# Conditioning summed along rows of output channels, with its products placed behind the weight tiles' low halves

## The chip, the cores and the metric

The kernel runs on one core of one Trainium2 chip. The metric is the device time of one execution in microseconds (us); lower is better. Inputs and output are float32 in the chip's main memory.

## The reference, cut to what matters

One decoder layer on 256 tokens of 2048 channels. A vector `c` (one per sequence) conditions it through a 2048 x 12288 matrix `w_ada`: six rows of 2048 values, which are a shift, a scale and a gate for each of the two sub-layers.

```python
mod = silu(c) @ w_ada + b_ada            # 6 x 2048: shift, scale, gate, shift, scale, gate
h = layer_norm(x) * (1 + mod[1]) + mod[0]
proj = h @ w_in                          # 2048 -> 9760 columns, in one product
...                                      # sparse attention and matrix memory on parts of proj
x = layer_norm(ALPHA * x + mod[2] * (merged @ w_o))
h = layer_norm(x) * (1 + mod[4]) + mod[3]
a, g = split(h @ w_up)
x = layer_norm(ALPHA * x + mod[5] * ((silu(dwconv(a)) * g) @ w_down))
```

The first norm inside each sub-layer has no gain and bias; the one after the residual has them.

## The kernel before, in words

Every weight tile is 128 partitions x 1024 float32 (512 KB; 392 KB for the `w_in_a` tiles of 784 columns). `load` issues it on SP's queue into one of the buffers of tile `w`; `load_split` then makes two halves of it for TensorE's reduced float32: ScalarE casts the high half (`wh`, line 96), VectorE subtracts to get the low half (`wl`, line 97). Each product is three matmuls: high by high, high by low, low by high. There are 4 buffers each of `wh` and `wl` and, before the change, 6 of `w` (`WB`).

**Conditioning.** `w_ada` is 192 such tiles, 32 for each of the six rows. A tile of `w_ada` holds 128 *input* channels on its partitions and 1024 outputs in its columns. VectorE multiplies each tile by one value per partition and adds it to an accumulator `acc` (line 157, one dependent chain of 16 tiles), after which TensorE sums over the partitions: for shifts and scales by matmuls against ones into `ps_ada`, for gates into `ps_adar`. The first 512 channels' shift and scale go straight from `ps_ada` into `modc` (one value per partition and chunk); later ones are copied to a row by ScalarE and moved onto the partitions by two small DMAs (`raw<-row`). So that a chunk is ready in this layout, channels are taken in a turned order: chunk 4 q + i, partition p is channel 512 q + 4 p + i. The transposes of the normalised input (`turn`) and the second norm's output `n2` therefore read or write with a stride of four elements.

**Input projection.** The 16 chunks of 128 input channels are taken in four groups of four. In each group the kernel runs over all columns of `w_in`: 24 blocks of 128 columns by `mm_b` (bank `ps_b`), then six ranges of 392 or 512 columns by `mm_a` (`ps_a`). A group has 24 weight tiles, 6 for each chunk. Its results are copied out by ScalarE in group 0 and added to the earlier ones by VectorE in the later groups. A group can begin only when shift and scale of its chunks are known and `hm` (ScalarE, line 299), the high cast of `hT` (ScalarE, 301) and its low half (VectorE, 302) are made.

**Ticker.** All other conditioning is spread over the weight tiles: after each weight tile `tk.tick(rate)` runs that many steps of a queue of generators; a step loads one `w_ada` tile and adds it to `acc` at once. During group g the ticker prepares group g + 1, one tile after each of the first weight tiles. The second sub-layer's shift and scale (64 tiles) start in group 3, the gates (32 tiles each) in the branch projections and in the channel mixer.

What is written here fixes the work and its data flow; a scheduler then sets the order in which the instructions stand in each engine's queue. Each engine takes its queue in order. `manual_schedule` around the norm between the sub-layers keeps VectorE's and ScalarE's written order there.

After the input projection come the merge gates' products, which fill the time between the steps of attention and matrix memory, the branch projections, the output projection, two norms, and the channel mixer in two halves (`ps_up`, `ps_d`).

Of the kernel before, what the change touches and what calls it, by code (L numbers as in the profile page):

```python
# [14 lines left out]
P = 128  # L15
S = 256
# [16 lines left out]
GR = (1.0, 1.0)  # L33
# [3 lines left out]
WB = (6, 4, 4)  # L37
NG0 = 8
FIRST = 14
F0 = 1  # L40
PTV = 2
YA, YB = 1, 2
# [9 lines left out]
def build(ctx: ExitStack, tc: tile.TileContext, d, out, dbg=None):  # L52
# [15 lines left out]
    nc.sync.dma_start(cst, d["cst"])  # L68
    ident = cst[:, C_ID:C_ID + P]
# [20 lines left out]

    def load_split(src):
# [5 lines left out]
        nc.vector.tensor_sub(wl[:, :n], t[:, :n], wh[:, :n])  # L97
        return wh, wl
# [24 lines left out]
    def rstd_steps(var, out_ap, n, nm):  # L123
        """1/sqrt(var + EPS), with a Newton step after the table's square root."""
# [20 lines left out]
    # ---------------------------------------------------------------- conditioning  # L145
# [4 lines left out]
    def ada_partial(u):  # L150
        acc = p0.tile([P, 1024], F32, name="acc", tag="acc")
        for k in range(KD):
            t = load(d["w_ada"][u * KD + k])
            if k == 0:
                nc.vector.tensor_scalar(acc, t, cs[:, 0:1], None, op0=ALU.mult)
            else:
                nc.vector.scalar_tensor_tensor(acc, t, cs[:, k:k + 1], acc, op0=ALU.mult, op1=ALU.add)  # L157
            if k < KD - 1:
                yield
        yield acc  # L160

    def ada_cols(u, m_sh, m_sc, q):
        """Shift and 1 + scale of the channels 512 q + 4 p + i, on partition p, in column 4 q + i."""
        for acc in ada_partial(u):
            if acc is None:
                yield
        for _ in range(YA):
            yield
        ps = bank(psa, "ps_ada")
        if q == 0 and m_sh == 0:  # L170
            src = [ps[:, 4 * i:4 * i + 4] for i in range(2)]
            for i in range(2):
                v = acc[:, i * 512:(i + 1) * 512].rearrange("k (c b) -> k b c", b=4)
                for b in range(4):
                    mm(src[i][:, b:b + 1], v[:, b, :], ones[:, 0:1], True, True)
        else:
            raw = p0.tile([P, 2, 4], F32, name="raw", tag="raw", bufs=2)
            for i in range(2):
                mm(ps[32 * i:32 * i + 32, :], ones[:, 0:32], acc[:, i * 512:(i + 1) * 512], True, True)
            row = t2([64, 512], "row")  # L180
            nc.scalar.copy(row, ps[0:64, :])
            for i in range(2):
                nc.scalar.dma_start(raw[:, i, :], row[32 * i:32 * i + 1, :])
            src = [raw[:, i, :] for i in range(2)]
            for _ in range(YB):
                yield
        for i, m in ((0, m_sh), (1, m_sc)):
            c0 = m * KD + 4 * q
            nc.vector.tensor_add(modc[:, m, 4 * q:4 * q + 4], src[i],
                                 prm[:, R_BADA + c0:R_BADA + c0 + 4])  # L190
        nc.vector.tensor_scalar(modc[:, m_sc, 4 * q:4 * q + 4], modc[:, m_sc, 4 * q:4 * q + 4],
                                1.0, None, op0=ALU.add)
        yield

    def ada_rows(u, dst, col, c):
        """1024 gate values on every partition."""
        for acc in ada_partial(u):
            if acc is None:
                yield
        for i in range(2):  # L200
            c0 = c * 1024 + i * 512
            bt = t2([P, 512], "badar")
            nc.sync.dma_start(bt, d["b_ada"][0:1, col + c0:col + c0 + 512].to_broadcast([P, 512]))
            ps = bank(psa, "ps_adar")
            mm(ps, ones, acc[:, i * 512:(i + 1) * 512], True, True)
            nc.vector.tensor_add(dst[:, c0:c0 + 512], ps, bt)
        yield

    def run_all(g):
        for _ in g:  # L210
            pass

    class Ticker:
        def __init__(self):
            self.q, self.credit = [], 0.0
# [3 lines left out]

        def tick(self, n):  # L220
# [9 lines left out]
        def drain(self):  # L230
            while self.q:
# [5 lines left out]
    # ---------------------------------------------------------------- input norm  # L237
# [4 lines left out]
    xt = p0.tile([P, 2, D], F32, name="xt", tag="t16")  # L242
    for t in range(2):
        for c in (0, 1024):
            nc.sync.dma_start(xt[:, t, c:c + 1024], d["x"][t * P:(t + 1) * P, c:c + 1024])
# [22 lines left out]
    first = ada_cols(0, 0, 1, 0)  # L268
    for _ in range(FIRST):
        next(first)  # L270
# [10 lines left out]
    def turn(p):  # L281
        ps = bank(psa, "ps_nT")
        for i in range(2):
            for t in range(2):
                q, b = divmod(2 * p + i, 4)
                v = xt[:, t, q * 512:(q + 1) * 512].rearrange("s (c b) -> s b c", b=4)
# [919 lines left out]
```

## Time and profile before

| | us |
|---|---|
| median of 3 runs | 1524.73 |
| lowest, highest run | 1518.71, 1528.0 |
| span of the profiled execution | 1516.5 |
| TensorE busy in it | 1457.4 |
| VectorE busy | 1112.6 |
| ScalarE busy | 727.0 |

For the profiled execution the page gives its span, from the first to the last instruction, and no time of its own beside it; the median of the runs is 8.2 us above that span, the lowest run 2.2 us.

The page's first part gives each engine's busy time, the second the span in 40 slices, the fourth the chain of work that ended last, followed back from the end. A share of busy time is an average over stages with different limits, so the questions that matter are which engine runs without a break in a given stretch and what ends its breaks; a matmul's end is modelled, so that counts of matmuls over a stretch say more than TensorE's busy share.

### The profile page before, as it was taken

To read this page: it belongs to the slowest core of one execution; us is meant where nothing else is said; L and a number is where in the kernel's file an instruction comes from. 1 tells how busy PE (TensorE), PEld (TensorE's weight loads), DVE (VectorE), ACT (ScalarE), POOL (GpSimd) and SP (SyncE) were. 2 spreads that over 40 slices of the span, in tenths; PEclk is the share of its full clock that TensorE was granted. 3 is DMA by queue.
4 is the path that set the end of the run, shared out by engine and by line. 5 is a ranking of instruction groups with operands and counts; after the bars stand their busy time and mean duration, and the time that the engine had idled before them with its cause. 6 is when DMAs were issued, how large, how long until landed. Compare 5 with 4: busy or idle time off the path is not lost.

```text
span 1516.5 us, 23668 instructions
## 1 busy us (share of the span) xinstructions
PE 1457.4 (96%) x9174; PEld 1299.5 (86%) x9174; DVE 1112.6 (73%) x1478; ACT 727.0 (48%) x1031; POOL 2.1 (0%) x6
## 2 busy tenths in 40 slices
PE   1999999999999999999699999999999999999997
PEld 1999898888889999988688888888898888888887
DVE  7869896897868778868877888865556666665557
ACT  3663443556565443434465455553335555554341
POOL 0000000000000000000000000000000000000000
PEclk9999999999999999999899999999999999999999
DMA  9989888894858899998358888866666666666662
GB/s 365 324 284 333 290 316 274 304 339 134 313 160 309 284 324 330 330 355 298 138 184 279 281 287 275 275 186 192 195 192 195 187 188 185 188 184 191 192 196 87
DMA packets 106961, 376.98 MB, mean 249 GB/s; under 512 B 13792, under 2 KB 13920, under 8 KB 106080
## 3 DMA queue, kind: packets, MB, share of 16 engines
q1 hardware_dynamic: 104832, 375.43, 73.9%
q8 instruction: 72, 1.18, 0.3%
q10 hardware_dynamic: 2016, 0.03, 0.1%
q14 instruction: 41, 0.34, 0.1%
HBM read 373.29 MB, written 2.10 MB: 248 GB/s over the span
## 4 chain that ended last, share of the span: by engine, by line
PE 89%; DVE 6%; DMA 2%; issue 1%; ACT 1%; DVEq 0%; SPq 0%; ACTq 0%
PE ps_up L77 33%; PE ps_d L77 16%; PE ps_mg L77 12%; PE ps_b L77 7%; PE ps_br L77 6%; PE ps_o L77 5%; PE ps_a L77 5%; DMA w<-in_w_ada_dram 2%; DVE acc L157 2%; DVE wl L97 1%; PE ps_y L77 1%; PE ps_s L77 1%; PE ps_ada L77 1%; PE ps_hid L77 1%; DVE xz L890 1%
## 5 line engine op out<-in xcount | busy, mean ns | idle before, releaser
L96 ACT CAST wh<-w 128x1024 fp32r<-128x1024 f32 (+1 forms) x478 | 495.9, 1038 | 571.4 <-PE ps_d L77 124.0
L97 DVE TENSOR_TENSOR wl<-w,wh 128x1024 fp32r<-128x1024 f32 (+1 forms) x478 | 575.4, 1205 | 255.1 <-ACT wh L96 254.7
L77 PE MATMUL ps_up<-h2T,wh 128*128 128x512 f32 x1408 | 496.5, 398 | 0.0
L77 PE MATMUL ps_up<-h2T,wl 128*128 128x256 f32 x1408 | 393.7, 280 | 0.0
L77 PEld LDWEIGHTS ps_up<-h2T,wh 128*128 128x128 f32 x1408 | 265.1, 188 | 64.3 <-ACT wh L96 0.5
L157 DVE SCALAR_TENSOR_TENSOR acc<-w,cs,acc 128x1024 f32<-128x1024 f32 x180 | 230.7, 1282 | 56.5 <-DMA w<-in_w_ada_dram 55.0
L77 PEld LDWEIGHTS ps_up<-h2T,wl 128*128 128x128 f32 x1408 | 266.0, 189 | 0.6 <-issue 0.5
L77 PE MATMUL ps_d<-wh,uTt 128*128 128x512 f32 (+1 forms) x792 | 210.4, 354 | 0.0
L77 PE MATMUL ps_mg<-hT,wh 128*128 128x256 f32 x1024 | 192.4, 287 | 0.0
L77 PEld LDWEIGHTS ps_mg<-hT,wh 128*128 128x128 f32 x1024 | 161.8, 193 | 5.7 <-issue 4.9
L77 PEld LDWEIGHTS ps_d<-wh,uTt 128*128 128x128 f32 x792 | 140.4, 189 | 20.8
L77 PE MATMUL ps_mg<-hT,wl 128*128 128x256 f32 x512 | 146.1, 285 | 0.0
L77 PE MATMUL ps_b<-hT,wh 128*128 128x256 f32 x768 | 140.4, 284 | 1.4 <-ACT hT L301 0.7
L77 PE MATMUL ps_d<-wl,uTt 128*128 128x512 f32 (+1 forms) x396 | 140.0, 354 | 0.0
L77 PEld LDWEIGHTS ps_b<-hT,wh 128*128 128x128 f32 x768 | 119.9, 192 | 5.9 <-issue 3.9
L77 PE MATMUL ps_b<-hT,wl 128*128 128x256 f32 x384 | 108.6, 283 | 0.6 <-DVE wl L97 0.6
L77 PE MATMUL ps_a<-wh,hT 128*128 128x392 f32 (+1 forms) x384 | 109.1, 359 | 0.0
L77 PEld LDWEIGHTS ps_mg<-hT,wl 128*128 128x128 f32 x512 | 98.6, 193 | 0.8 <-issue 0.7
L77 PEld LDWEIGHTS ps_d<-wl,uTt 128*128 128x128 f32 x396 | 74.9, 189 | 10.3
L77 PEld LDWEIGHTS ps_a<-wh,hT 128*128 128x128 f32 x384 | 71.0, 188 | 10.0 <-issue 2.7
L77 PEld LDWEIGHTS ps_b<-hT,wl 128*128 128x128 f32 x384 | 73.6, 192 | 1.2 <-DVE wl L97 0.8
L77 PE MATMUL ps_a<-wl,hT 128*128 128x392 f32 (+1 forms) x192 | 68.6, 358 | 0.0
(248 smaller groups left out, 1400.6 us busy)
## 6 DMA issues: line engine op xcount, KB each, us to landing
w<-in_w_ada_dram SPq DMA_DIRECT2D x192, 512.0 KB, 4.9
w<-in_w_up_dram SPq DMA_DIRECT2D x176, 512.0 KB, 4.2
w<-in_w_down_dram SPq DMA_DIRECT2D x90, 512.0 KB, 3.9
w<-in_w_mg_dram SPq DMA_DIRECT2D x64, 512.0 KB, 5.0
w<-in_w_in_b_dram SPq DMA_DIRECT2D x48, 512.0 KB, 5.0
w<-in_w_br_dram SPq DMA_DIRECT2D x32, 512.0 KB, 5.4
w<-in_w_o_dram SPq DMA_DIRECT2D x32, 512.0 KB, 5.5
w<-in_w_in_a_dram SPq DMA_DIRECT2D x32, 392.0 KB, 4.3
```

The source lines that it names most:

```text
L77: nc.tensor.matmul(o, lhsT, rhs, start=start, stop=stop)
L96: nc.scalar.copy(wh[:, :n], t[:, :n])
L97: nc.vector.tensor_sub(wl[:, :n], t[:, :n], wh[:, :n])
L157: nc.vector.scalar_tensor_tensor(acc, t, cs[:, k:k + 1], acc, op0=ALU.mult, op1=ALU.add)
L890: nc.vector.scalar_tensor_tensor(z, z, mv[:, 0:1], lg[:, c * 512:(c + 1) * 512], op0=ALU.subtract, op1=ALU.mult)
```

## The change: layout and sum, groups, placing, buffers

1. `w_ada` is stored transposed: a tile now holds 128 *output* channels on its partitions and half of the 2048 input channels in its columns. `crow` holds silu(c) along the free axis, the same on every partition; 16 transposes and 4 ScalarE copies make it at the start. One VectorE instruction multiplies a tile by half of `crow` and sums along the columns (`accum_out`) into `parts`. Two halves and the bias are added, and `modc` is there: no `acc` chain, no `ps_ada`, no small DMAs. A chunk of 128 channels is ready after 4 tiles (shift and scale, two halves each).
2. Channels are taken in plain order: the strides of four in `turn` and `second_norm` go.
3. The gates come out per partition too. After two more ticks (`YA`) they are spread by 8 transposes of 128 columns and 2 ScalarE copies per 1024 gates; before it was two ones matmuls of 512 columns in two passes each, a bias load and two VectorE additions.
4. The groups of the projection are 3, 4, 5 and 4 chunks. The rate of the ticker in a group is set so that the `w_ada` tiles of the next group are spread evenly over all its weight tiles (16 over 18, 20 over 24, 16 over 30).
5. A tick now loads the tile; the product is written at the next tick, after that weight tile's low half, and `behind` forbids the scheduler to move it in front of that.
6. `w` has 8 buffers. The input `x` is loaded ahead of everything but the constants, as it already was in the queue.

```diff
+GROUPS = (3, 4, 5, 4)
-WB = (6, 4, 4)
+WB = (8, 4, 4)
...
+        lows.append(nc.vector.tensor_sub(wl[:, :n], t[:, :n], wh[:, :n]))
...
+        nc.tensor.transpose(ps[:, j * P:(j + 1) * P], cs[:, 4 * i + j:4 * i + j + 1].to_broadcast([P, P]),
+                            ident)
+    nc.scalar.copy(crow[:, i * 512:(i + 1) * 512], ps)
...
+    def ada_chunk(m, k):
+        for i in range(2):
+            t = load(d["w_ada"][(m * KD + k) * 2 + i])
+            def products(t=t, i=i):
+                ins = nc.vector.scalar_tensor_tensor(
+                    t, t, 1.0, crow[:, i * 1024:(i + 1) * 1024], op0=ALU.mult, op1=ALU.mult,
+                    accum_out=parts[:, m, k, i:i + 1])
+                if lows:
+                    behind(ins, lows[-1])
+            yield products
...
+        def last():
+            products()
+            o, v = modc[:, m:m + n, k0:k1], parts[:, m:m + n, k0:k1, :]
+            nc.vector.tensor_add(o, v[:, :, :, 0], v[:, :, :, 1])
+            nc.vector.tensor_add(o, o, bada[:, m:m + n, k0:k1])
+            if then:
+                then()
...
+    def ada_mod(k0, k1):
+        while k0 < k1:
+            k = min(k0 + 2, k1)
+            yield from ada_cols(0, 2, k0, k, lambda k0=k0, k=k: modulate_in(k0, k))
+            k0 = k
+    run_all(ada_mod(0, GROUPS[0]))
...
         def tick(self, n):
+            self.flush()
             self.credit = self.credit + n if self.q else 0.0
             while self.credit >= 1 and self.q:
                 self.credit -= 1
                 try:
-                    next(self.q[0])
+                    f = next(self.q[0])
+                    if f:
+                        self.late.append(f)
...
+    for gi, kn in enumerate(GROUPS):
+        nxt = gi < len(GROUPS) - 1
+        if nxt:
+            tk.add(ada_mod(k0 + kn, k0 + kn + GROUPS[gi + 1]))
+            rate = 4 * GROUPS[gi + 1] / (6 * kn)
...
     def second_norm(t, c):
-        z = xz[:, t, c * 512:(c + 1) * 512].rearrange("s (c b) -> s c b", b=4)
-        o = n2[:, t, c * 512:(c + 1) * 512].rearrange("s (b c) -> s c b", b=4)
+        z, o = xz[:, t, c * 512:(c + 1) * 512], n2[:, t, c * 512:(c + 1) * 512]
```

How the instructions move, at three places.

SP's queue at the start, before:

```order
L245 DMA xt<-in_x_dram 128x1024 x4
L88 DMA w<-in_w_ada_dram 128x1024 x6
L407 DMA gb<-in_ml_gate_b_dram 128x8
L88 DMA w<-in_w_ada_dram 128x1024 x10
L88 DMA w<-in_w_in_b_dram 128x1024
L88 DMA w<-in_w_ada_dram 128x1024
L88 DMA w<-in_w_in_b_dram 128x1024
```

The same place with the change:

```order
L72 DMA xt<-in_x_dram 128x1024 x4
L92 DMA w<-in_w_ada_dram 128x1024 x8
L415 DMA gb<-in_ml_gate_b_dram 128x8
L92 DMA w<-in_w_ada_dram 128x1024 x4
L92 DMA w<-in_w_in_b_dram 128x1024 x2
L92 DMA w<-in_w_ada_dram 128x1024
L92 DMA w<-in_w_in_b_dram 128x1024
```

The first weight tile moves from the 17th to the 13th place among the large tiles.

ScalarE's queue where group 0 ends and group 1 begins, before (the numbers at `ps_a` are banks; the last range of group 0 is 917 and 918):

```order
L96 CAST wh<-w 128x1024
L299 ACTIVATE hm<-nT,modc 128x256 x4
L301 CAST hT<-hm 128x2x256
L96 CAST wh<-w 128x1024
L301 CAST hT<-hm 128x2x256
L530 COPY projA<-ps_a_872 128x2x256
L530 COPY projA<-ps_a_873 128x2x256
L96 CAST wh<-w 128x1024 x2
L530 COPY projA<-ps_a_917 128x2x256
L530 COPY projA<-ps_a_918 128x2x256
```

With the change (the last range of group 0 is 772 and 773):

```order
L537 COPY projA<-ps_a_732 128x2x256
L537 COPY projA<-ps_a_733 128x2x256
L107 CAST wh<-w 128x1024
L537 COPY projA<-ps_a_772 128x2x256
L107 CAST wh<-w 128x1024
L537 COPY projA<-ps_a_773 128x2x256
L310 ACTIVATE hm<-nT,modc 128x256 x2
L107 CAST wh<-w 128x1024
L312 CAST hT<-hm 128x2x256
```

All four chunks of group 1 were modulated ahead of group 0's last copies; now its last two chunks are modulated behind the copy of group 0's last bank.

VectorE's queue at the same place with the change:

```order
L108 TENSOR_TENSOR wl<-w,wh 128x1024
L180 SCALAR_TENSOR_TENSOR w,parts<-w,crow 128x1024 x2
L108 TENSOR_TENSOR wl<-w,wh 128x1024
L198 TENSOR_TENSOR modc<-parts 128x2x2
L108 TENSOR_TENSOR wl<-w,wh 128x1024
L199 TENSOR_TENSOR modc<-modc,prm 128x2x2
L108 TENSOR_TENSOR wl<-w,wh 128x1024
L180 SCALAR_TENSOR_TENSOR w,parts<-w,crow 128x1024
L313 TENSOR_TENSOR hT<-hm,hT 128x2x256
```

The last two products of group 1's conditioning stand behind group 0's last low half (the first row), and the low half of `hT` behind three low halves of group 1.

## Rows read from the trace of the kernel before

**Rows 1.** Windows: stretch, its us, busy us (instructions) by engine, PEclk, DMA share, GB/s.

```profile
0.00:45.70 45.70, 11.39 (x52) 10.02 (x52) 34.23 (x51) 18.08 (x29) 1.16 (x5) 1.00 0.95 355
45.70:80.00 34.30, 34.30 (x286) 34.30 (x287) 27.82 (x25) 18.26 (x26) 0.00 (x0) 1.00 0.94 334
327.00:465.90 138.90, 138.77 (x931) 117.74 (x931) 105.99 (x177) 81.48 (x178) 0.00 (x0) 0.98 0.66 232
```

**Rows 2.** The chain that ended last, in order: start us, us, what.

```profile
33.57 1.30 DVE acc L157
34.91 3.90 PE ps_ada L77 x16
...
40.27 2.08 ACT hm L299 x4
...
88.70 0.98 PE ps_ada L77 x4
...
173.91 34.57 PE ps_b L77 x286
208.48 14.10 PE ps_a L77 x79
...
237.70 7.67 PE ps_b L77 x64
...
406.55 0.87 PE ps_pT L684 x8
...
567.89 1.72 PE ps_adar L77 x4
```

**Rows 3.** Timeline, start and joint of groups 0 and 1: start us, us, engine, line.

```profile
17.73 17.13 DVE L157 SCALAR_TENSOR_TENSOR acc<-w,cs,acc 128x1024 f32<-128x1024 f32 x13
...
33.78 1.05 ACT L96 CAST wh<-w 128x1024 fp32r<-128x1024 f32 x1 [12.05 <-DMA w<-in_w_in_b_dram]
...
109.16 0.40 PE L77 MATMUL ps_b<-hT,wh 128*128 128x256 f32 x2
```

**Rows 4.** VectorE from 109 to 174 us, by shape: busy us, mean ns, idle before.

```profile
L97 DVE TENSOR_TENSOR wl<-w,wh 128x1024 fp32r<-128x1024 f32 x16 | 19.4, 1219 | 0.0
L157 DVE SCALAR_TENSOR_TENSOR acc<-w,cs,acc 128x1024 f32<-128x1024 f32 x15 | 19.2, 1283 | 5.1 <-DMA w<-in_w_ada_dram 5.0
L97 DVE TENSOR_TENSOR wl<-w,wh 128x784 fp32r<-128x784 f32 x8 | 7.7, 975 | 0.0
...
L501 DVE TENSOR_TENSOR accM<-ps_b,accM 128x512 f32<-128x512 f32 x4 | 2.8, 691 | 0.0
...
L302 DVE TENSOR_TENSOR hT<-hm,hT 128x512 fp32r<-128x512 f32 x2 | 1.3, 684 | 0.0
...
L189 DVE TENSOR_TENSOR modc<-raw,prm 128x4 f32<-128x4 f32 x2 | 0.3, 158 | 4.5 <-DMA raw<-row 4.5
```

**Rows 5.** The norm between the sub-layers, 738 to 774 us, by shape.

```profile
L890 DVE SCALAR_TENSOR_TENSOR xz<-xz,mv_z,lnr 128x512 f32<-128x512 f32 x8 | 5.9, 741 | 0.0
L922 ACT ACTIVATE sqj<-xz,sq 128x512 f32<-128x512 f32 x8 | 5.6, 707 | 6.2 <-DVE sq L920 6.2
L895 DVE SCALAR_TENSOR_TENSOR xz<-xz,mv_z,lnr 128x512 f32<-128x512 f32 x8 | 5.6, 742 | 0.0
...
L947 ACT ACTIVATE n<-xz,mv_n 128x512 f32<-128x512 f32 x4 | 5.1, 1272 | 0.0
...
L895 DVE DVE_READ_ACCUMULATOR xz<-xz,mv_z,lnr 128x1 f32 x8 | 0.7, 82 | 0.0
```

**Rows 6.** ScalarE over the whole program, by shape.

```profile
L299 ACT ACTIVATE hm<-nT,modc 128x256 f32<-128x256 f32 x16 | 8.3, 593 | 4.3 <-DVE modc L191 4.3
...
L301 ACT CAST hT<-hm 128x512 fp32r<-128x512 f32 x8 | 4.8, 618 | 0.0
...
L530 ACT COPY projA<-ps_a 128x512 f32<-128x512 f32 x4 | 2.2, 588 | 1.1 <-PE ps_a L77 1.0
```

**Rows 7.** DMA from 16 to 34 us: packets, MB, mean rate.

```profile
DMA packets 2153, 7.32 MB, mean 407 GB/s; under 512 B 367, under 2 KB 367, under 8 KB 2153
```

More of the change, by code (lines that the diff above doesn't have):

```diff
@@ L68, in build @@
     nc.sync.dma_start(cst, d["cst"])
+    xt = p0.tile([P, 2, D], F32, name="xt", tag="t16")
+    for t in range(2):
+        for c in (0, 1024):
+            nc.sync.dma_start(xt[:, t, c:c + 1024], d["x"][t * P:(t + 1) * P, c:c + 1024])
     ident = cst[:, C_ID:C_ID + P]
@@ L89, in load, with behind @@
         return t
+    lows = []
+    def behind(ins, other):
+        tc.add_manual_dep(ins.ins, other.ins.name, mybir.DependencyInfo(
+            mybir.DependencyClass.NoSync, mybir.DependencyReason.DATA), reason="order")
     def load_split(src):
@@ L148, in build @@
     modc = p0.tile([P, 6, KD], F32, name="modc")
[L150 to L166, printed above, removed]
+    parts = p0.tile([P, 6, KD, 2], F32, name="parts")
+    bada = prm[:, R_BADA:R_BADA + 6 * KD].rearrange("p (m k) -> p m k", m=6)
+    for m in (1, 4):
+        nc.vector.tensor_scalar(bada[:, m, :], bada[:, m, :], 1.0, None, op0=ALU.add)
+    crow = p0.tile([P, D], F32, name="crow")
+    for i in range(4):
+        ps = bank(psm, "ps_c")
+        for j in range(4):
+            nc.tensor.transpose(ps[:, j * P:(j + 1) * P], cs[:, 4 * i + j:4 * i + j + 1].to_broadcast([P, P]),
+                                ident)
+        nc.scalar.copy(crow[:, i * 512:(i + 1) * 512], ps)
@@ new lines, in ada_chunk, with ada_cols @@
+    def ada_chunk(m, k):
[8 more added lines that the diff above has]
+            yield products
+    def ada_cols(m, n, k0, k1, then=None):
+        for k in range(k0, k1):
+            for i in range(n):
+                for j, products in enumerate(ada_chunk(m + i, k)):
+                    if (k, i, j) != (k1 - 1, n - 1, 1):
+                        yield products
+        def last():
[5 more added lines that the diff above has]
+                then()
+        yield last
@@ L167, in ada_cols, with ada_rows @@
+    def ada_rows(m, dst, c):
+        yield from ada_cols(m, 1, 8 * c, 8 * c + 8)
         for _ in range(YA):
             yield
[L169 to L199, printed above, removed]
@@ L467, in gate_steps, with stream @@
         yield
-    for gi in range(4):
-        nxt = gi < 3
+    def stream(src, width, per):
+        tiles = iter(range(src.shape[0]))
+        while True:
+            wh, wl = load_split(src[next(tiles)][:, :width * per])
+            work()
+            for i in range(per):
+                yield wh[:, i * width:(i + 1) * width], wl[:, i * width:(i + 1) * width]
+    wb, wa, wv = (stream(d[n], w, p) for n, w, p in (("w_in_b", P, 8), ("w_in_a", AW, 2), ("w_in_v", 512, 2)))
+    k0 = 0
+    for gi, kn in enumerate(GROUPS):
+        nxt = gi < len(GROUPS) - 1
         if nxt:
-            tk.add(ada_mod(gi + 1))
+            tk.add(ada_mod(k0 + kn, k0 + kn + GROUPS[gi + 1]))
+            rate = 4 * GROUPS[gi + 1] / (6 * kn)
+        else:
+            rate = GR1
         comp = []
```

179 lines of the change are left out of this document (72 added, 107 removed).

## The prediction

> **What bounds the kernel now.** I read the windows first, then the chain in order of time, then timelines at the places where the chain leaves TensorE. In the windows TensorE is busy through every stretch from 45.7 us on, bar the norm between the sub-layers and the tail; the 45.7 us before the first full-rate matmul are the one large hole (11.4 us busy) [rows 1]. The reader should see in the chain that the hole ends in four steps in line: the last of 16 conditioning sums, starting at 33.57; 16 matmuls into `ps_ada`, 34.91 to 38.8; the modulation `hm` from 40.27; and only then `ps_b` [rows 2].
>
> The projection groups begin at 45.7, 109.16, 173.91 and 237.70 [rows 1 to 3], so they last 63.5, 64.8 and 63.8. What must TensorE alone have? 286 matmuls of `ps_b` take 34.6 us, and the `ps_a` part from 208.48 to 237.70 takes 29.2, of which 0.98 is a `ps_ada` pair [rows 2]: 62.8 us a group, 15.7 a chunk. The groups are thus TensorE bound to within 1 us each (1.0 of real stall, in the second). A change can win only the start, work taken off TensorE, and little else; it can lose at the joints of the groups.
>
> **The change, part by part.** Times are against the profiled span of 1516.5 us; the median of the runs is 8.2 us above it, and I carry that over.
>
> *Start.* 13 sums last 17.13 us, a pace of 1.318 [rows 3]; four fewer tiles bring the last start from 33.57 to 28.3, its end to 29.6. Behind it stand one low half of `hT` (0.68) and two tiny additions (0.16 each) [rows 4]: 30.6. Then two weight low halves of 1.22 [rows 4] and one half-size low half (about 0.4): the third chunk is complete at about 33.5. The weights are no later: the first cast at 33.78 [rows 3] was of the 17th large tile, now it is the 13th, 4 x 1.318 earlier, 28.5. By 33.5 TensorE has 21 matmuls of chunks 0 and 1 behind it, 2.5 us at 34.6/286 each: it is as if it had run without a break from 31.0. Before, that point is 45.7 less three early matmuls, 45.3. The gain is 14.3. The new `crow` copies, four of about 0.59 (as a 512-column copy, [rows 6]), stand on ScalarE before the input norm's root; I give back 1.3 and take **-13.0**, bounds -14.5 (copies hidden before the first tile) and -9 (the sums paced by something later, four tiles saved and only half of the `ps_ada` step).
>
> *Off TensorE in the groups.* Three `ps_ada` pairs of 0.98 [rows 2]: **-2.9**. The 1.0 of stall is counted again below, so **-1.0** here.
>
> *Joints.* This is the price. The last `w_ada` tiles now come with the last weight tiles of a group, not with the 16th of 24. At the first joint, with E the end of group 0 on TensorE, ScalarE's queue holds: copy, cast, copy, two `hm`, cast, cast of `hT`. From E: cast 1.05, copy 0.59; `hm` waits for VectorE's second low half and addition, 1.05 + 1.22 + 0.16 = 2.4, then 2 x 0.59; cast 1.05; `hT` 0.62: 5.3 us. VectorE then has low half, product and `hT`'s low half: 4.65 + 1.22 + 1.28 + 0.68 = 7.8 [rows 3, 4, 6]. TensorE has 23 matmuls for these 7.8 us, 2.8 us: **+5.0**. At the second joint VectorE has after E one addition of a bank (0.69), a low half, a product and `hT`'s low half, 3.9; TensorE has 2.6 to do; with the odd fifth chunk 0.7 more is lost: **+2.0**. At the third all products and both halves of the additions stand before the last banks' copies, `hT` is whole at E + 2.1, and 21 matmuls (2.5 us) cover it: **0**. Bounds for the three together: 0 (the scheduler's order with everything earlier than E) and +12 (each as the first, less what covers the third).
>
> *Transfers and VectorE in the groups.* Group 0 needs 28 tiles of 0.524 MB and 6 of 0.401: 17.1 MB. At the 334 GB/s of a busy stretch [rows 1] that is 51 us, at the 407 of the start [rows 7] 42, against 47.1 of TensorE; loads begin some 4 us before TensorE. **+1.0**, bounds 0 and +5. VectorE in group 1: 16 and 8 low halves 27.3, 20 products of 1.283 + 0.082 27.3, 24 bank additions of at most 0.69 16.6, the rest 2.6: 73.8 by mean durations against 62.8. But in the 65 us of rows 4 the like sum is 19.4 + 7.7 + 19.2 + 16.6 + 2.6 = 65.5 with 9.6 of waits beside it: some 80 neighbours overlap by 0.13 each, and 88 in the new group 1 make 73.8 into 63. Hidden, just; the cover is the four `wl` buffers, and without them it costs up to 5.
>
> *The product with a sum.* No conditioning product in this trace has `accum_out`. The nearest rows are the norm's: 742 ns with it, 741 without, and 82 ns for the read of the accumulator [rows 5]. I take 1.283 + 0.08. The Trainium skill (Vector Engine (DVE) Microarchitecture Reference, Points that are easy to get wrong) says that this shape of instruction with two float32 sources in SBUF runs at half throughput, for want of a port to the accumulator; by it each product would be 2.6 us. The trace disagrees for 512 columns: 742 against 741.
>
> *After the groups.* Four `ps_ada` pairs less, one of which I count as hidden in attention's waits: 3 x 0.98. Four gate spreads of 1.72 become 8 transposes, 0.87 as the eight of `ps_pT` [rows 2]: 4 x 0.85. **-6.3**, bounds -7.4 and -3 (if only the branch stage gives it). Attention: the generators lose their idle steps (80 ticks become 64 for the second shift and scale), so some 9 more tiles fall into 327 to 466 us, 12 us of VectorE on 106 of 139 [rows 1]. A product there can delay a softmax step: **+1.0**, bounds -2 and +4. Norm: ScalarE's strided 1272 ns should be near the 707 of a plain one [rows 5]; of four, two stand on the chain: **-1.0**, bounds 0 and -2.5. Channel mixer: same tiles, TensorE bound, nothing.
>
> Sum: -13.0 - 2.9 - 1.0 + 7.0 + 1.0 - 6.3 + 1.0 - 1.0 = **-15.2**: span 1501.3, time 1524.73 - 15.2 = **1509.5**.
>
> **Rivals.**
> 1. *The start's gain is given back at the joints* (0.25). Each group's shift and scale are now just in time; if transfers hold 334 GB/s and the joints cost 12, the sum is -15.2 + 5 + 4 = -6, up to -3: 1518 to 1522. For: the 51 us against 47.1. Against: `w` tiles now wait in 8 buffers, and VectorE's waits for `w_ada` (5.0 in rows 4) should go.
> 2. *The joints are hidden* (0.17): TensorE reaches them with a backlog, because ScalarE and VectorE stall it elsewhere or the early chunks last. Then -15.2 - 7 - 1 = -23: 1501.5.
> 3. *Slower: the product with a sum is slow* (0.03). At 2.57 us, 12 products lengthen the start by 15; group 0's VectorE goes from about 44 to 65 us against 47, group 1's from 63 to 89 against 63, group 2's by 8 past its 78.5; attention, where VectorE already has 106 of 139 us [rows 1], and the stages behind it lose 15 more. About +82 on the forecast, 1590. The gain is gone from about 1.65 us a product on. Against it stand the 742 and 741; for it, that those rows are 512 columns and multiply by a column. It is the rule above that would do this.
> 4. *Slower by some other displacement of the order*, in attention above all (0.05): 1525 to 1540.
>
> **How the numbers follow.** The sum's own case (0.50) spans 1504 to 1515. Faster than 1509.5 by chance half of it, and rival 2. One per cent, 15 us, is about what a measurement here tells from no change. Faster by over 1%: 0.25 + 0.17 = 0.42, and a little of rival 1's and the mixed cases' luck, 0.44; slower by over 1%, past 1540: rival 3 and part of 4, with the cases between, 0.06; within 1%: 0.50. The range leaves out rivals 3 and 4 and the ends of 1 and 2: 1499 to 1523.
>
> **What would show it.** First `ps_b` near 29 and unbroken running from 33 or 34 us (if past 37, the start is mis-sized). Group starts near 79 + 5, 147 and 229 us; waits of TensorE for `hT` at the first two joints and none at the third. A product of 1.28 us with a read of 0.08; if it is over 1.6, rival 3 holds. No `ps_ada`; `ps_adar` at 0.87 per 1024 gates. `n` at about 0.7. Attention's length, from the first merge gate to the first branch matmul, within 3 us of before. The forecast is wrong if the groups together take over 200 us, or if VectorE shows no gap in groups 0 and 1.

## The result

The changed kernel took 1510.6 us, the median of four executions from 1501.8 to 1512.2; the kernel before, executed beside it, 1521.9 us. The ratio is 0.990, 95% interval 0.986 to 0.994. Forecast were 1509.5 us and a ratio of 0.990. The profiled execution took 1510.55 us, with a span of 1508.5 us where the forecast had 1501.3; so total and ratio came out as forecast and the span of this one execution 7 us longer. The stages say why. Each number is a start on TensorE's timeline or the distance between two of them (us); the last column is a second profile of the same program, which took 1502.97 us.

| stretch | before | forecast of the difference | changed | changed, second profile |
|---|---|---|---|---|
| first `ps_b` | 44.35 | about -15 | 30.63 | 29.77 |
| start of the last group | 237.54 | -8.5 (near 229 us) | 228.29 | 226.51 |
| last group, to the first merge-gate product | 77.83 | | 76.60 | 76.60 |
| attention 1, to the first `ps_n` (gates, mLSTM heads) | 28.81 | | 40.08 | 33.02 |
| attention 2, to the branch product behind its last cast | 121.58 | both +1.0 | 125.66 | 125.13 |
| branch stage, to the first `ps_o` | 188.90 | -6.3, for all stages behind the groups | 181.14 | 181.13 |
| output projection and norm | 106.31 | -1.0 | 104.74 | 104.74 |
| up 1; down 1 | 252.66; 121.50 | 0 | 252.51; 121.55 | 254.21; 121.55 |
| up 2 | 248.75 | 0 | 245.62 | 245.62 |
| down 2 and the end of the span | 132.6 | 0 | 132.3 | 132.3 |

The groups came out at the size that the prediction gave. Attention lost 15.4 us where 1.0 was forecast, and the branch stage and the second up projection gained more than forecast.

### The profile page after: what moved, and what is told of

Its sections match the earlier page's. It is cut to its first block, busy times and chain, and to the rows that moved or that the text cites. A ratio compares the mean times of both kernels' runs of the same rounds, so it can differ in the third digit from the quotient of the medians.

```text
span 1508.5 us, 23486 instructions
## 1 busy us (share of the span) xinstructions
PE 1455.5 (96%) x9162; PEld 1304.5 (86%) x9162; DVE 1104.6 (73%) x1669; ACT 727.0 (48%) x1037; POOL 2.1 (0%) x6
## 4 chain that ended last, share of the span: by engine, by line
PE 92%; DVE 4%; DMA 1%; ACT 1%; issue 1%; SPq 0%; DVEq 0%
PE ps_up L81 33%; PE ps_d L81 16%; PE ps_mg L81 12%; PE ps_b L81 9%; PE ps_br L81 6%; PE ps_a L81 6%; PE ps_o L81 5%; PE ps_y L81 1%; DVE w L180 1%; PE ps_s L81 1%; DVE xz L898 1%; DVE xz L903 1%; PE ps_hid L81 1%; DVE wl L108 1%; DMA xt<-in_x_dram 1%
## 5 line engine op out<-in xcount | busy, mean ns | idle before, releaser
L180 DVE SCALAR_TENSOR_TENSOR w<-w,crow 128x1024 f32<-128x1024 f32 x192 | 233.0, 1219 | 0.0
L81 PE MATMUL ps_mg<-hT,wh 128*128 128x256 f32 x1024 | 188.2, 284 | 0.0
```

Of the source, the lines that this page charges most:

```text
L81: nc.tensor.matmul(o, lhsT, rhs, start=start, stop=stop)
L180: ins = nc.vector.scalar_tensor_tensor(t, t, 1.0, crow[:, i * 1024:(i + 1) * 1024], op0=ALU.mult, op1=ALU.mult, accum_out=parts[:, m, k, i ...
```

## The profile after

Windows of the changed kernel, with the columns of [rows 1]: start, group 0, joint 1, group 1, the mLSTM heads, the end of the attention.

```profile
0.00:31.90 31.90, 10.95 (x53) 9.03 (x53) 23.41 (x56) 19.41 (x31) 1.16 (x5) 0.96 0.95 352
31.90:80.00 48.10, 48.10 (x320) 46.52 (x321) 39.30 (x54) 29.12 (x45) 0.00 (x0) 0.96 0.98 363
80.00:92.00 12.00, 9.62 (x50) 8.53 (x49) 7.63 (x12) 5.92 (x9) 0.00 (x0) 0.72 0.93 340
92.00:153.00 61.00, 59.88 (x411) 57.24 (x409) 60.60 (x93) 25.86 (x30) 0.00 (x0) 1.00 0.95 341
326.00:345.00 19.00, 19.00 (x56) 13.30 (x57) 6.54 (x15) 4.16 (x10) 0.00 (x0) 0.50 0.29 105
452.00:471.40 19.40, 13.70 (x67) 9.09 (x65) 5.12 (x9) 11.61 (x16) 0.00 (x0) 0.82 0.34 121
```

The hole at the start is 31.9 us instead of 45.7 [rows 1]. Group 0's loads run at 363 GB/s, against 334, and TensorE has no idle time in it. Three places then show either idle time or a granted clock under 1: joint 1, the heads (0.50 throughout, the lower of the two levels, 1.2 GHz) and the attention's end.

The chain of the changed kernel, start us, us and what, as [rows 2]:

```profile
30.63 1.22 PE ps_b L81 x4
31.89 24.79 PE ps_b L81 x192
...
84.61 34.34 PE ps_b L81 x263
...
152.94 40.11 PE ps_b L81 x337
...
228.45 8.71 PE ps_b L81 x74
...
602.69 0.87 PE ps_adar L213 x8
```

The 16 `ps_ada` matmuls and the rows behind them are gone. TensorE runs unbroken from 31.89, from 84.61 after joint 1, from 152.94 after joint 2, and passes joint 3 without a wait; a gate spread costs 0.87 us instead of 1.72.

Joint 1 on the changed kernel's timeline, and in the last row joint 2: start us, us, engine, line, and in brackets the idle time before and what ended it.

```profile
80.11 1.05 ACT L107 CAST wh<-w 128x1024 fp32r<-128x1024 f32 x1
...
81.19 1.23 DVE L108 TENSOR_TENSOR wl<-w,wh 128x1024 fp32r<-128x1024 f32 x1 [0.78 <-ACT wh L107]
81.21 0.51 PE L81 MATMUL ps_b<-hT,wh 128*128 128x256 f32 x2 [0.69 <-ACT wh L107]
...
82.33 0.16 DVE L199 TENSOR_TENSOR modc<-modc,prm 128x4 f32<-128x4 f32 x1
...
82.53 1.09 ACT L310 ACTIVATE hm<-nT,modc 128x256 f32<-128x256 f32 x2 [0.88 <-DVE modc L199]
...
83.52 1.03 ACT L107 CAST wh<-w 128x1024 fp32r<-128x1024 f32 x1
84.46 0.61 ACT L312 CAST hT<-hm 128x512 fp32r<-128x512 f32 x1
...
84.61 1.32 PE L81 MATMUL ps_b<-hT,wh 128*128 128x256 f32 x4 [1.41 <-ACT wh L107]
85.73 1.22 DVE L180 SCALAR_TENSOR_TENSOR w<-w,crow 128x1024 f32<-128x1024 f32 x1
...
86.87 0.69 DVE L313 TENSOR_TENSOR hT<-hm,hT 128x512 fp32r<-128x512 f32 x1
...
152.94 0.39 PE L81 MATMUL ps_b<-hT,wh 128*128 128x256 f32 x1 [0.89 <-DVE hT L313]
```

It is the queue that the prediction wrote out, in that order: E is 80.1, `hm` waits for the addition `modc`, and the low half of `hT` stands behind a weight's low half and a product. What TensorE waits for is something else: it stops for 0.69, 0.28 and 1.41 us, each time for a half of a weight tile. The last of these, the cast of 83.52, stands on ScalarE behind `hm`. For `hT` it does not stop at all here (0.5 us in the second profile); joint 2 has that wait, 0.89 us. At 84.61 four matmuls take 1.32 us where two take 0.40 at full clock [rows 3]: after the wait TensorE has half the clock until about 91 us, so that three matmuls start every 0.64 us instead of 0.35. The prediction had the queue, but neither the wait for the cast nor the clock.

VectorE from 31 to 80 us by shape, and ScalarE in the norm from 738 to 774 us (busy us, mean ns):

```profile
L180 DVE SCALAR_TENSOR_TENSOR w<-w,crow 128x1024 f32<-128x1024 f32 x16 | 19.4, 1219 | 0.0
...
L180 DVE DVE_READ_ACCUMULATOR w<-w,crow 128x1 f32 x16 | 1.3, 83 | 0.0
```

```profile
L954 ACT ACTIVATE n<-xz,mv_n 128x512 f32<-128x512 f32 x4 | 3.2, 804 | 0.0
```

The product with a sum costs 1219 ns and 83 for the read; back to back the products start 1.14 us apart, against 1.318 for the accumulating chain of before [rows 3]. `n` fell from 1272 to 804 ns [rows 5].

The attention's end in the changed kernel, ScalarE and TensorE:

```profile
455.80 1.04 PE L692 MATMUL ps_pT<-cst,pt 128*128 128x128 f32 x8
456.20 1.28 ACT L801 ACT_TABLE_LOAD   x1
...
457.49 3.62 ACT L801 ACTIVATE gates<-gates 128x4096 f32<-128x4096 f32 x1
461.01 0.57 ACT L622 COPY pT<-ps_pT 128x512 f32<-128x512 f32 x1
461.63 2.07 PE L81 MATMUL ps_y<-pT,projA 128*128 128x512 f32 x2 [4.80 <-ACT pT L622]
```

This is a wait that the prediction did not have. The transposes are done at 456.8, their copy stands on ScalarE behind the sigmoid over all eight stored merge gates, and TensorE waits 4.80 us and then runs at half clock. In the kernel before the same sigmoid (table load at 467.4) came after the attention: there the last merge-gate product, which fills TensorE's time, started at 465.64, 4.5 us behind the attention's last `ps_y` product, here at 452.80, 17 us before that product's end. So the gates were complete 13 us sooner, and the sigmoid stands in the queue where they were ready. That the planner (the scheduler that sets the order) put it there for this reason is read from the order and not shown.

## The experiments

Each is the changed kernel with the edit shown; the kernel before ran beside all of them.

### The change once more

No edit.

> The changed kernel once more, unaltered, as the measure for the others on the same chip. Its four executions so far took 1510.55, 1501.77, 1510.61 and 1512.23 us. Theory 1, a lottery of the granted clock: the stretch of the four ml_weights heads, which ran at 0.50 in the profiled execution of the change, ran at 0.89 in the profile of the kernel with the sigmoid moved, with the same instructions in the same order up to there, and took 7 us less; so the executions fall into two heaps 7 to 10 us apart, near 1502 and 1510, and a profile of the lower heap shows a clock over 0.8 from 328 to 346 us. Theory 2, plain spread: no heaps, all within 4 us of one median, and the clock in that stretch is 0.5 again.

Measured: 1508.72 us median of six, 1501.3 to 1512.2 (ratio 0.991, 0.988 to 0.994). Windows of the profiled execution (1502.97 us) and, under it, of the first profile of the same program (1510.55 us):

```profile
328.00:334.00 6.00, 6.00 (x26) 4.33 (x24) 2.48 (x7) 0.79 (x3) 0.00 (x0) 0.76 0.22 84
334.00:340.00 6.00, 6.00 (x42) 5.68 (x42) 3.83 (x10) 2.78 (x6) 0.00 (x0) 1.00 0.16 35
340.00:346.00 6.00, 6.00 (x41) 5.61 (x40) 5.09 (x21) 2.81 (x6) 0.00 (x0) 1.00 0.66 219
```

```profile
328.00:334.00 6.00, 6.00 (x22) 4.52 (x21) 2.94 (x9) 1.76 (x5) 0.00 (x0) 0.50 0.61 200
334.00:340.00 6.00, 6.00 (x16) 4.00 (x16) 1.32 (x3) 0.73 (x2) 0.00 (x0) 0.50 0.00 0
340.00:346.00 6.00, 6.00 (x21) 4.67 (x20) 1.27 (x3) 1.66 (x3) 0.00 (x0) 0.50 0.00 0
```

The kernel before has the half clock at this place too:

```profile
328.00:334.00 6.00, 6.00 (x35) 4.67 (x34) 5.96 (x8) 2.32 (x5) 0.00 (x0) 0.84 0.98 384
334.00:340.00 6.00, 6.00 (x22) 4.42 (x21) 5.22 (x11) 2.47 (x5) 0.00 (x0) 0.59 0.99 361
```

It lasts from 332 to 339 us there, from 324 to 331 in the second profile of the change and from 322.5 to 346.5 in the first; so the change did not bring it, but it can last longer. The two profiles of the change have the same instructions in the same order, and the stretch to the first `ps_n` takes 33.02 or 40.08 us. That is 7.06 of the 7.7 us between the two spans. The ten executions lie at 1501.3 to 1503.0 (three), 1507.0 (one) and 1510.4 to 1512.2 (six): theory 1, but for the one between. So of attention's loss 7 us belong to the clock of an execution and are not there in every one. What is left between the 28.81 us of before and 33.02 are some 32 more merge-gate products ahead of the first `ps_n`, about 3.8 us at 11.52 for 96, which the stretch behind it no longer has.

### The sigmoid behind the attention

```
+        tails.append(nc.scalar.copy(hi, src))          # nsa_out, last cast
-    nc.scalar.activation(gates0, gates0, AF.Sigmoid)
+    behind(nc.scalar.activation(gates0, gates0, AF.Sigmoid), tails[-1])
```

> The change, with the one sigmoid over the eight stored merge gates (128x4096, table load 1.28 us and 3.62 us) put behind ScalarE's last cast of the attention instead of ahead of its last four pT copies; nothing else differs until then. Theory 1, the sigmoid stands in the way: TensorE waited 4.80 us for the pT copy at 461.01 us and then ran at half clock, so the first unbroken branch product (471.36 us in the changed kernel) comes 5 to 8 us earlier, near 464 to 466 us, and the total falls from 1510.6 to 1503 to 1506 us. Theory 2, the attention's last part is bound by the chain of transposes, copies and ps_y products itself: the wait only moves to another copy, the branch product comes at most 1.5 us earlier, and the total stays within 2 us of 1510.6. Theory 3, the sigmoid is only moved ahead of the branch's weight casts: the attention ends 5 us earlier and the first branch tiles lose the same 4.9 us, total 1510.6 again.

Measured: 1500.63 us (1495.8 to 1505.7), ratio 0.988 (0.985 to 0.990). From the first `ps_n` to the branch product behind the last cast 118.36 us, against 125.66 and 125.13: 7.3 and 6.8 gained, the branch stage unchanged at 181.13. The window of the attention's end:

```profile
455.00:475.00 20.00, 19.10 (x156) 18.66 (x156) 13.93 (x21) 13.02 (x12) 0.00 (x0) 1.00 0.53 183
```

The same window of the changed kernel:

```profile
455.00:475.00 20.00, 14.30 (x70) 9.69 (x70) 3.25 (x5) 10.51 (x12) 0.00 (x0) 0.83 0.20 66
```

Theory 1: the 4.9 us of ScalarE cost 7, since TensorE now keeps its clock (1.00 instead of 0.83). Its mark for the branch product, 464 to 466 us, was overshot with 455.92, since the heads took 33.04 us in this profile and not 40.08. Of the six executions three lie in its range for the total (1503.6 to 1505.7) and three 8 us below it (1495.8 to 1497.7). Theory 3 falls: the branch tiles lose nothing. What is left of attention's loss is 33.04 + 118.36 - 28.81 - 121.58 = +1.0 us. It can be named: 24 branch products that now stand in the attention (2.9 us) less two `ps_ada` pairs that are gone from it (2.0).

### Fewer products per merge-gate tile

```
-RATES = (1.2, 0.8, 0.3)
+RATES = (0.96, 0.8, 0.3)
```

> The change, with 0.96 instead of 1.2 conditioning steps per merge-gate tile in the attention: the rate at which the kernel before in effect issued them, since some of its steps were empty. The stretch from the first merge-gate product to the first unbroken branch product took 166.3 us in the changed kernel and 150.4 before. Theory 1, density: the denser conditioning loads and sums keep merge-gate tiles and the attention's own vector work waiting; the stretch comes back to 150 to 156 us, and the total to 1496 to 1502 us, less what the products pushed into the branch stage cost there (up to 2 us). Theory 2, order: what was lost hangs on where the merge-gate products and the four ml_weights heads stand in TensorE's order (half clock from 326 to 345 us) and on the sigmoid ahead of the last pT copies, and a fifth fewer products mends neither except by accident: the stretch stays at 161 us or more, total 1506 to 1514 us. Theory 1's mark is VectorE's or the transfers' share above 0.9 in the stretches that shrink; in the changed kernel they were 0.25 to 0.79 there, which speaks for theory 2.

Measured: 1501.90 us (1499.1 to 1511.6), ratio 0.989 (0.986 to 0.991); both attention stretches 155.7 us, 37.88 + 117.83. By the numbers theory 1, but its mark is missing, and the order changed: the heads' stretch holds 28 more merge-gate products than in the second profile above (33.02 us), and the copy behind the sigmoid kept TensorE waiting 3.4 us, not 4.8. Undecided by itself; the kernel with all three edits, further on, settles it.

### One product per weight tile in the groups

```
-            rate = 4 * GROUPS[gi + 1] / (6 * kn)
+            rate = 1.0
```

> The change, with one product per weight tile in projection groups 0 to 2 instead of 0.89, 0.83 and 0.53 spread evenly to the group's end, so that the last product of the next group's scales is done 2, 3 and 8 tiles ahead of the joint. Theory 1, joints: at joint 1 TensorE waited from 80.1 to 84.6 us for the new hT and then ran at half clock until about 91 us (some 7 us in all), at joint 2 0.9 us; both go, the last group starts at 221 to 223 us instead of 228.45, and the total falls by 5 to 7 us to 1504 to 1506. Theory 2, transfers: in group 0 the 16 queues are 0.97 busy, so a product earlier is a weight tile later; TensorE waits for tiles ahead of the joint for what it no longer waits at it, the last group starts within 2 us of 228.45 and the total stays within 3 us of 1510.6. Theory 3, VectorE: it is 60.6 of 61 us busy in group 1, so the denser products there push the low halves back: the joints are gone but group 1 grows by 2 to 5 us.

Measured: 1504.59 us (1502.2 to 1508.2), ratio 0.990 (0.988 to 0.992). The last group starts at 224.68. Joint 1 and the waits inside group 1:

```profile
78.00:94.00 16.00, 15.76 (x119) 14.76 (x118) 14.58 (x20) 9.35 (x13) 0.00 (x0) 1.00 1.02 384
94.00:144.00 50.00, 48.84 (x318) 44.94 (x317) 49.13 (x78) 21.56 (x27) 0.00 (x0) 1.00 0.95 346
```

Joint 1 is gone (idle 0.2 us, clock 1.00). TensorE waits 1.1 us for halves of weight tiles at the end of group 0 and 1.2 us for low halves in group 1 instead. Over the profiles with the spread pace and the written order the last group starts at 226.5 to 229.4 (five), with pace 1 at 224.3 to 224.9 (three, this one and two below): 3.6 us by the means, about half of what the joints cost. Theory 1 has the mechanism, theory 3 the half that is given back; the total does not show it, since the sigmoid's wait (4.8 us) is still there.

### Both repairs

The edits of the sigmoid and of the pace.

> The change with two repairs at once: the stored gates' sigmoid behind the attention's last cast, and one product per weight tile in groups 0 to 2. Theory 1, they add: the sigmoid gave 7.3 us from the first ps_n product to the first branch product behind the attention, the pace 3.6 us at the last group's start; together 11 us under the unaltered change of this call in executions of like clock, 1491 to 1499 us. Theory 2, they overlap: the pace moves the attention's order, the tail in the kernel with the pace alone was bound by other waits (clock 0.84 from 440 to 455 us, TensorE 10.2 of 15 us busy), and the two together give no more than the sigmoid alone, 1496 to 1505.

Measured: 1494.88 us (1493.2 to 1495.9), ratio 0.982 (0.979 to 0.985): faster than both kernels. The last group starts at 224.31, the attention takes 34.24 + 118.66 us. 13.8 us under the median of the change beside it, in theory 1's range and under theory 2's. In executions of like clock the gain is less than the 11 us that theory 1 adds up: 6 to 8 us under the change's faster executions, 7.1 between the spans of the two profiles (2.2 at the last group's start, 5.2 in the attention). So they add, in part. Its five executions lie within 2.7 us; why none of them is 7 us slower, as executions of the change are, is not shown.

### Both repairs and fewer products

All three edits above.

> The change with the sigmoid behind the attention's last cast, one product per weight tile in groups 0 to 2, and 0.96 instead of 1.2 conditioning steps per merge-gate tile in the attention. Theory 1, density: fewer products in the attention leave it faster by 3 us or more than the kernel with the first two alone (from the first merge-gate product to the first branch product behind the attention 152.9 us there), total 1488 to 1492. Theory 2, order only: the density was never the cost, the stretch stays within 2 us of 152.9 and the total within 3 us of 1494.9, and a stretch above it shows products that now miss the branch stage's or the attention's cover.

Measured: 1493.26 us (1492.3 to 1498.6), ratio 0.982 (0.980 to 0.984). The attention takes 152.3 us against 152.9 with the repairs alone, with a like clock in the heads (0.86 and 0.85): theory 2. The density of products was not the cost.

### Six load buffers

```
-WB = (8, 4, 4)
+WB = (6, 4, 4)
```

> The change, with 6 load buffers as before instead of 8. Theory 1, the two buffers carry something: a product's tile holds its buffer until VectorE has multiplied it in place, about one weight tile's time longer than a weight tile does, and with 6 buffers the loads of groups 0 and 1 start later; TensorE waits 3 to 8 us more for weight tiles in the groups and the total rises to 1513 to 1519. Theory 2, they carry nothing: the first loads are at the rate of the transfers anyway (0.94 to 1.03 busy up to 80 us) and later the share is under 0.96, so group starts move by less than 1 us and the total stays within 3 us, the order of the attention left aside, whose time is read apart.

Measured: 1507.39 us (1504.1 to 1515.4), ratio 0.992 (0.990 to 0.994). The last group starts at 229.34, and it takes 80.40 us where the profiles with eight buffers have 76.6 to 77.2; 1.70 of it is a wait for `gT` of the compressor and 1.0 one for its `hp`. So in this profile the buffers carry 3 to 4 us, in the last group, whose compressor tiles share them, and not where theory 1 put it; the start of the last group lies inside the spread of the other profiles (226.5 to 229.4). The total does not show it.

### Groups of four chunks

```
-GROUPS = (3, 4, 5, 4)
+GROUPS = (4, 4, 4, 4)
```

> The change with groups of 4, 4, 4, 4 chunks, as before, instead of 3, 4, 5, 4: the rows of channels, the placing and the buffers stay. Theory 1, the start: 16 tiles instead of 12 precede the first joint's hT, 4 more at 1.14 to 1.3 us each, so the first unbroken group 0 comes 4.5 to 5.3 us later; joint 1 moves 24 us later and its stall (4.5 us, then half clock) stays, since its last product still stands at the group's end; the last group starts at 231 to 234 us instead of 228.3. Theory 2, hidden: TensorE runs at half clock and waits for weight tiles until 36 us anyway, so the later start costs 1 us or less, and the longer group 0 has VectorE and transfers less full (0.67 products per tile instead of 0.89): joint 1 or 2 shrinks and the last group starts at 225 to 228 us.

Measured: 1505.10 us (1500.5 to 1509.4), ratio 0.989 (0.986 to 0.992). The first `ps_b` starts at 36.88, 6 to 7 us later; but there is no wait for `hT` at any joint, and the last group starts at 229.37, in neither theory's range and at the late end of the unequal groups' 226.5 to 229.4. Both theories are half right: unequal groups win the start and pay most or all of it back at joint 1. By the last group's start that part of the change is worth 0 to 3 us; the total does not show it.

### Without the written order of the products

```
-                if lows:
-                    behind(ins, lows[-1])
```

> The change without the order that it writes out (each product behind the latest weight tile's low half): the planner is free to put a product on VectorE ahead of that low half. Theory 1, the order protects TensorE: with it gone a low half waits out a product of 1.14 us more often, which TensorE feels where VectorE is full (60.6 of 61 us in group 1), and the last group starts 1 to 5 us later than 228.3 us. Theory 2, the order costs as much as it brings: at joint 1 the last sum stood behind a low half (1.2 us) and it now comes earlier, so joint 1 shortens by about 1 us and the last group starts at 226 to 228 us. Total within 5 us of the unaltered change either way; read by the start of the last group, since the attention's order shifts too.

Measured: 1531.22 us (1530.0 to 1537.1), ratio 1.007 (1.004 to 1.010): neither theory. In the groups theory 2 was right, and by more than it said: the last group starts at 222.05. But behind it the kernel loses, against the second profile of the change, 11 us in the attention, 11.5 in the branch stage (192.68) and 12 in up 1. Waits of TensorE for low halves from 760 to 1030 us, waits of VectorE for the products' tiles in the attention (us in total, times, longest), and one of the first on the timeline:

```profile
PE ps_up L81 <- DVE wl L108: 10.5, 8, 1.7
```

```profile
DVE w L180 <- DMA w<-in_w_ada_dram: 27.4, 18, 3.7
```

```profile
944.35 1.23 DVE L180 SCALAR_TENSOR_TENSOR w<-w,crow 128x1024 f32<-128x1024 f32 x1 [1.67 <-DMA w<-in_w_ada_dram]
...
945.50 1.22 DVE L108 TENSOR_TENSOR wl<-w,wh 128x1024 fp32r<-128x1024 f32 x1
...
946.77 0.38 PE L81 MATMUL ps_up<-h2T,wl 128*128 128x256 f32 x1 [1.04 <-DVE wl L108]
```

A product whose tile has not landed (VectorE waits 1.67 us for the DMA) stands ahead of a low half that could go, and TensorE waits. Such waits of VectorE come to 27.4 us in the attention, 44.0 in the branch stage and 52.2 in up 1; with the written order there are none in these stretches, in either profile of the change. The order is worth 22 us here, and the prediction gave it no term.

### The written order only behind the groups

With the sigmoid's repair:

```
-                if lows:
+                if lows and m > 1:
```

> The change with the sigmoid behind the attention's last cast, and the written order of products (behind the latest low half) kept only for the modulation rows 2 to 5, which are multiplied from the last group on; in groups 0 to 2 the planner places the products itself. Theory 1, the order has two faces: without it the last group started at 222.05 us instead of 226.51 (its last sums come earlier at the joints), but in the branch stage and the first up projection products whose tile had not landed stood ahead of ready low halves, and TensorE waited 7 and 10.5 us for them. Then the last group starts at 221 to 223 us here, the branch stage takes 181 us again, the first up projection 252 to 254, and the total is 1490 to 1497 us. Theory 2, the loss of 22 us comes from the groups' order as it carries on into the attention: the total stays above 1505.

Measured: 1504.63 us (1498.4 to 1508.7), ratio 0.988 (0.986 to 0.990). The branch stage takes 182.62 and up 1 253.06, so the losses of the kernel above are gone there, and VectorE's waits for products' tiles with them. The last group starts at 223.38. But the total missed theory 1's range: the attention takes 166.4 us, against 151.4 with the sigmoid's repair alone. 6 of these 15 us lie in the heads (39.40 against 33.04), at half clock as in the first profile of the change (0.60 from 316 to 346). The others lie behind them, where the merge-gate products are used up at 439 us and TensorE waits 4.1 us for a softmax step of VectorE. So theory 2 falls for the branch stage and up 1, and not for the attention: what the groups' order changes there stays open.

### The same with one product per tile

> As the kernel before this one, with one product per weight tile in groups 0 to 2 as well. Theory 1, the two repairs of the joints do the same thing and don't add: joint waits are already under 1.5 us, so the last group starts at 221 to 224 us and the total lies within 3 us of the other kernel's. Theory 2, they add: another 2 to 4 us, last group at 218 to 220 us.

Measured: 1503.36 us (1500.3 to 1510.3), ratio 0.989 (0.987 to 0.991). The last group starts at 225.46, 1.5 us outside theory 1's range on the late side, the attention takes 158.4: the two joint repairs do not add.

### The heads apart

On the kernel with the sigmoid's repair:

```
         Ws.append(ml_weights(h))
-        fill(1)
+        fill(2)
```

> The kernel with the sigmoid behind the attention's last cast (six executions in two heaps, 1495.8 to 1497.7 and 1503.6 to 1505.7 us), with two merge-gate tiles instead of one called between the ml_weights heads, so that 18 and 32 merge-gate products stand on TensorE where 6 and 1 stood, between the third and fourth head and behind the fourth. Theory 1, the half clock comes from the heads' short products standing close together: spread out, the granted clock from 316 to 346 us stays over 0.85 in the profile, the executions fall in one heap (within 4 us), and no gain against the lower heap is left but for tiles that the tail then lacks: 1495 to 1500 us. Theory 2, the fall is set by what TensorE does before the heads (the 32 products of 16 columns and the gate steps ahead of them), which this leaves alone: the clock falls to 0.5 in some executions again, two heaps 7 to 9 us apart, median 1497 to 1506 us.

Measured: 1506.80 us (1501.6 to 1510.0), ratio 0.991 (0.989 to 0.993), where the kernel without this edit has 0.988 (0.985 to 0.990): no gain, and perhaps a loss of some 4 us.

```profile
322.00:328.00 6.00, 6.00 (x37) 4.89 (x37) 6.00 (x11) 3.09 (x4) 0.00 (x0) 0.78 1.03 412
328.00:334.00 6.00, 6.00 (x21) 4.52 (x21) 3.30 (x9) 1.76 (x5) 0.00 (x0) 0.50 0.95 376
334.00:340.00 6.00, 6.00 (x37) 5.00 (x37) 2.39 (x4) 1.78 (x3) 0.00 (x0) 0.87 0.00 0
```

The clock falls at 325 us, at the end of the 32 products of 16 columns that stand ahead of the heads (321.94 to 325.89); in the profiles of before and of the change it falls during them or within 2 us behind them. It is back at 335.5. From 316 to 346 us it is 0.83 in the mean, and the executions spread over 8 us. Theory 1 falls, and the attention's end lacks the tiles (used up at 439 us). Theory 2 has the place of the fall, but there are no two clear heaps and the median lies above its range. Why the clock comes back early in one execution and late in another is open.

## Why the prediction was right, step by step

**Start, -13.0: right.** Unbroken running began at 31.89 instead of 45.69, 13.8 us, of which the half clock until 36 us takes some 1.5 (192 matmuls in 24.79 us, at the pace of [rows 2] 23.2): 12.3.

**Transfers, +1.0, and VectorE in group 1, hidden:** TensorE had no wait in group 0, so nothing of the first; VectorE was busy 60.6 of 61 us in group 1, hidden but just, as forecast.

**Joints, +7.0: right in size and queue, by another wait.** Forecast were 5.0, 2.0, 0. At joint 1 TensorE was idle 2.4 us, and the half clock up to 91 us took some 3 more, about 5.4 in all; at joint 2 it waited 1.1 us, at joint 3 not at all. Forecast was a wait of 5.0 for the low half of `hT` at joint 1; measured were waits for weight halves behind `hm`, half as long, and a clock that the prediction did not have. That the sizes agree there is luck. The start of the last group, 228.29, was forecast as 229. Rival 2 (joints hidden) is what groups of four chunks or pace 1 give, and there it costs the start or new waits; rival 1 (the gain eaten) did not happen: 9.3 us of it were left at the last group.

**The product with a sum, 1.283 + 0.08: right.** 1.219 + 0.083. The Trainium skill (Vector Engine (DVE) Microarchitecture Reference, Points that are easy to get wrong) would, as the prediction reads it, have had it at half throughput, by its estimate 2.6 us. 1219 ns for 1024 columns, like the 1224 of a plain subtraction of that shape, contradict this here too. An instruction with one source of that shape is faster (750 ns, line 155 of the kernel before), so a second source costs time, with or without the sum.

**After the groups, -6.3: right kind, more found.** The last group gained 1.2 and the branch stage 7.8. Of the 7.8, 24 branch products (2.9 us) had only moved into the attention; a `ps_ada` pair is gone (1.0), and of two gate spreads of 1.72 one of 0.87 is left, the other having moved into the output projection (2.6); merge-gate blocks of 96 matmuls ran in 11.30 instead of 11.52 us, eight of them, 1.8, whose cause is open. Some 0.5 is lost at the stage's start, where the first two products take 0.73 us.

**Attention, +1.0: the step that failed, +15.4.** The prediction looked for VectorE's denser products; the kernel with all three edits shows that these cost nothing that can be seen. What it lacked is (a) the gates' sigmoid ahead of the last `pT` copies, since the merge-gate tiles are used up 17 us before the attention's end and not behind it: 7 us, shown by moving it; (b) half clock in the heads that lasts 24 us instead of 7: 7 us, shown by two executions of one program. Without both +1.0 is left, and that is branch products moved in and `ps_ada` pairs gone, no delayed softmax step. It named "some other displacement of the order", in attention above all, as a rival at 0.05, with a cost of 15 to 30, and the displacement was there at 7.

**Norm, -1.0**: -1.6. **Channel mixer, 0**: -3.1 in up 2. A pair of matmuls there starts every 0.349 us instead of 0.353, at a granted clock of 1.00 in both. The same two paces occur in up 1 of two executions of the changed program (252.51 and 254.21 us), so such a step needs no edit. But up 2 took 245.6 us in every profile of the change and its variants and 248.75 in the one of before: whether the change does it is open.

So the forecast span was nearly that of the second profile, 1500.8, and the forecast total carried over 8 us between the profile and the median of before, where both profiled executions of the change took 2 us more than their spans and the median of before was lower later (1521.9, 1519.4). That the total came out to 1 us is luck: it is the sum of right groups, an attention mis-sized by a wait and a clock, 3 to 6 us that came unforeseen elsewhere, and a base that was 3 to 5 us too high.

## What to carry to other kernels

Where a planner sets the order, ask of every filler when it now runs out, and which instruction becomes ready with its last tile: a long one (here a sigmoid over 4096 columns) lands on an in-order queue ahead of work that TensorE waits for, and here one written dependency moved it away. Give operations whose tiles may be late a place behind those that feed TensorE; taking that place away cost 22 us here, far from where it was looked for. Before explaining a difference of half a per cent, profile the same program twice.

## What the runs showed of the hardware

- Two waits of TensorE cost more than themselves. The 4.8 us at the attention's end cost 7, the 2.4 us of idle time at joint 1 some 5.4, both by the half clock behind them (0.83 and 0.72 in those windows). The 1.1 us at joint 2 did not: the clock stayed at 1.00 from 150 to 156 us.
- Half clock holds in a stretch that counts as fully busy: 6.00 of 6 us with 16 matmuls, at 0.50.
- The table load took 1.28 us, the sigmoid started 0.01 us after it, and the work ahead of it had ended 0.02 us before. The Trainium skill (ScalarE: Activation LUTs, What ACT_TABLE_LOAD costs) gives about 1283 ns, which agrees, and about 1380 ns of draining besides, which this trace does not show.
